# Entry of the down-projection: the order of VectorE's work on low parts of weights, a recombination, a product of convolutions and operands

## The chip, the cores and the metric

The kernel runs on one core of one Trainium2 chip. The metric is the device time of one execution in microseconds (us). Every engine of the core takes its instructions in the order in which the program was laid out for it: TensorE (PE; PEld is its weight load) multiplies matrices, VectorE (DVE) and ScalarE (ACT) work elementwise, GpSimd (POOL) too, and SyncE (SP) issues most transfers. An instruction that must wait for another engine holds up all that stands behind it on its own engine.

## The reference, cut to what matters

One layer of a decoder on 1024 tokens of width 1024. After the attention part, with `x` the residual stream:

```
xn = rmsnorm(x, norm_ffn_w)
u  = xn @ w_up                       # 1024 x 5632
c  = conv_b + sum_j upad[:, j:j+S] * conv_w[j]     # causal, width 3, per channel
gate, val = split(c, 2)
x  = x + (silu(gate) * val) @ w_down # 2816 -> 1024
return rmsnorm(x, norm_final_w)
```

All data are float32. The change touches the seam between `u`, `c` and the product with `w_down`.

## The kernel before, in words

The kernel holds everything transposed: channels on the 128 partitions, tokens along the free axis. A float32 product is made from three matmuls: each operand is split into a high part (a cast by ScalarE, `wh` for weights at line 139, `h` for activations at line 820) and a low part (the rest, by VectorE, `wl` at line 141 and `h` at line 821), and TensorE adds high x high, high x low and low x high.

**The up-projection** (`hidden`) goes over 22 pairs of output blocks j = 0 to 21; NF is 22. Each pair is made by seven products P1 to P7 of half the size, put together by VectorE in `recombine` (lines 460 to 467): `us` of the gate block and `us` of the value block come out of it. GpSimd multiplies `us` by the row scale of the norm (`scaled`, L1051), ScalarE and VectorE do the convolution (`conv`: L1065, L1067, L1068), ScalarE the silu (L1043), VectorE the product of gate and value (`glu`, L1044), and SyncE stores it in DRAM (`hd`, L1045). The work of the value block of the pair before the last, and of both blocks of the last pair, is kept in a list (`self.defer`) and done later, during the down-projection's first chains.

**The down-projection** (`down`) is again made of seven half-size products, the stages P1, P2, P5, P6, P3, P7 and P4. In every stage the 11 blocks k of the inner dimension are cut into six and five; for each cut there are four weights, one for each block of 128 output channels. So i counts 56 weights, and i = 0 to 3 are weights 1 to 4 of stage P1 with six k, i = 4 to 7 weights 5 to 8 with five k. For every weight there is one chain of matmuls (L1121): high x high, high x low, low x high for each k. The activations of P1's first six k are split ahead of it; those of the other five k and of all later stages are the "operands": they are read back from `hd` by `fetch_h` (L1003), combined and split into parts by `operand` while the chains run, two or so at a time. The list `preps` names them in order, and the table `count` says how many follow each weight.

Weights have three buffers as they come from DRAM (`raw`), and two each for the high and the low parts: the cast of weight n + 2 waits until chain n is done, and the load of weight n + 3 until the low part of weight n has been made. SyncE's queue carries, in one order, these loads (L129), the reads of `hd` (L1003), the stores into `hd` (L1045) and the loads of the residual (L1158), which VectorE adds to the chains' results (L1127).

What sets the order on an engine: a planner goes through the program and always issues, on each engine, the ready instruction of the highest priority by its own estimate of times; earlier in the text is higher, and `tc.high_priority(n)` lifts a block. `tc.issue_after(ins)` puts all that a block issues on the engine of `ins` behind `ins`. In this place:

```
with tc.high_priority(100):          # last pair, before its recombine: weights 1 and 2
    for k in range(6, HK):
        self.fetch_h("B11", k)
    self.ahead(2)
self.front = self.hi.ins, self.lo.ins
self.defer.pop(0)(lo)
```

`self.hi` and `self.lo` are the cast and the low part issued last, here those of weight 2; `front` puts the next convolution behind them. In `down`, `next_w` at weight i = 1 prepares weight 3, at i = 2 weight 4, and so on; the operands that follow it stand behind that weight's cast and low part. `DEFER = (2, 4)` and `STORE = (1, 6)` name the i at which the last pair's convolutions and the two late stores are done.

Of the kernel before, what the change touches and what calls it, by code (L numbers as in the profile page):

```python
# [13 lines left out]
ALU = mybir.AluOpType  # L14
# [10 lines left out]
NF = DFF // P  # L25
# [19 lines left out]
class Trunk:  # L45
# [405 lines left out]
                        self.keep(m, u, (tp, "hi"))  # L451
        self.uw = None

    def recombine(self, ps, us, tp, o):

        nc = self.nc
        c11, c12, c21, c22 = (us[w][:, o + hf * H2:o + (hf + 1) * H2] for w in range(2) for hf in range(2))
        s1, u2, u3, u4 = (self.tl(tp, [P, H2], n, bufs=1) for n in ("s1", "u2", "u3", "u4"))
        tt = nc.vector.tensor_tensor
        nc.scalar.copy(s1, ps["P1"])  # L460
        tt(c11, ps["P2"], s1, ALU.add)
        tt(u2, ps["P6"], s1, ALU.add)
        tt(u3, ps["P7"], u2, ALU.add)
        tt(c22, ps["P5"], u3, ALU.add)
        tt(u4, ps["P5"], u2, ALU.add)
        tt(c12, ps["P3"], u4, ALU.add)  # L466
        tt(c21, u3, ps["P4"], ALU.subtract)

    def keep(self, m, u, to):

# [77 lines left out]
    def store(self, dst, src):  # L548

        self.stores.append((dst, src))  # L550
# [353 lines left out]
    def hidden(self, pair):  # L904
        nc, tc = self.nc, self.tc
        with ExitStack() as ctx:
# [11 lines left out]
            for j in range(NF):  # L918
                w, ps = ready.pop(j) if j else (w0, {})
                if j == 0:  # L920
# [4 lines left out]
                    for k in range(4):  # L925
                        hi, lo = self.split(*(xc2.tile([P, T], F32R, name=f"T42_{k}{p}") for p in "hl"), self.t42[k])
                        self.B["T4", k], self.B["T2", k] = ((hi[:, c], lo[:, c]) for c in (slice(0, H2), slice(H2, T)))
                    self.tctx.close()
                    tp = e(tc.tile_pool(name="tp", bufs=2, side="right", reuse_waits="tile"))
# [7 lines left out]
                if j == NF - 1:  # L937
# [3 lines left out]
                    with tc.high_priority(50):  # L941
# [3 lines left out]
                        lo = self.lo  # L945
# [4 lines left out]
                us = [self.tl(tp, [P, T + 2], "us", bufs=3) for _ in range(2)]  # L950
                if j == NF - 1:
# [7 lines left out]
                        self.ahead(2)  # L959
                    self.front = self.hi.ins, self.lo.ins  # L960
                    self.defer.pop(0)(lo)
                self.recombine(ps, us, tp, 2)
                if j < NF - 1:

                    with nullcontext() if j else tc.issue_after(self.pow.ins):

                        w, ps = ready[j + 1] = self.next_w(), {}
# [68 lines left out]
    def glu(self, j, w, us, tp, after):  # L1036

        nc = self.nc
        c = self.conv(j + w * NF, us, tp, after)
        if w == 0:  # L1040
            self.c0 = c
            return
        nc.scalar.activation(self.c0, self.c0, AF.Silu)  # L1043
        nc.vector.tensor_tensor(self.c0, self.c0, c, ALU.mult)  # L1044
        store = lambda c0=self.c0: nc.sync.dma_start(self.hd[j], c0)  # L1045
        self.late.append(store) if after is not None else store()

    def scaled(self, m, us, after=None):
# [22 lines left out]
    def down(self):  # L1071

        nc, tc = self.nc, self.tc
        with ExitStack() as ctx:
# [5 lines left out]
            tt = nc.vector.tensor_tensor  # L1080
# [7 lines left out]
            def fetch(name, *ks):  # L1088
                for k in ks:
                    self.fetch_h(name, k)  # L1090

            def prep(c):
                for _ in range(c):
                    if preps and preps[0] not in (("P4", k) for k, _ in again):
                        stage, k = preps.pop(0)
                        self.operand(stage, k)
                        if stage == "P7":
                            again.append((k, None))
# [16 lines left out]
            def product(ps, w, stage, c, start, a=0, b=H2, each=None):  # L1115

                k0, k1 = CUTS[c]
                for k in range(k0, k1):
                    h, l = (t[:, a:b] for t in self.B[stage, k])
                    for i, (v, x) in enumerate(((w[0], h), (w[0], l), (w[1], h))):  # L1120
                        nc.tensor.matmul(ps, v[:, k - k0, :], x, start=start and k == i == 0, stop=k == HK - 1 and i == 2, skip_group_check=True)  # L1121
                    if each:
                        each(k)

            def evict(ps, m, hf, done):
                x = col(m, hf)
                tt(x, x, ps, ALU.subtract if m > 3 else ALU.add)  # L1127
                if done:
                    norm(m, hf)
# [7 lines left out]
                loads.setdefault(14 + k // 2, []).append(("B22", k))  # L1137
            for k in range(1, 6):
                loads[7 + k].insert(0, ("B11", k))
            count = {0: 3, 1: 2, 3: 1, 4: 1, 6: 2, 7: 2}  # L1140
            chains, owed, tail, i = [{}, {}], [], [], 0
            for stage in STAGES:
                which, start, o, hf, done = plan[stage]
                for c in range(2):
                    for m in range(4):
                        if stage == "P4" and c == 1 and m > 1:
                            break
                        with tc.high_priority(150 if i < 4 else 0), tc.issue_after(self.load.ins) if i == 1 else nullcontext():
                            w = self.next_w()
                        lo = self.lo  # L1150
                        if start and c == 0:
                            chains[which][m] = bank(which)
                        ps = chains[which][m]
                        product(ps, w, stage, c, start)
                        if i % 8 == 2 and i < 32:
                            r, h = ((0, 0), (4, 1), (0, 1), (4, 0))[i // 8]
                            with tc.issue_after(self.load.ins):
                                nc.sync.dma_start(x3[:, r:r + 4, h * H2:(h + 1) * H2], self.x2d[r:r + 4, :, h * H2:(h + 1) * H2].rearrange("m p t -> p m t"))  # L1158
                        for l in loads.get(i, ()):
                            fetch(*l)  # L1160
                        for k, _ in again:
                            fetch("B21", k)
                        again.clear()
                        with tc.issue_after(self.hi.ins), tc.issue_after(lo.ins):
                            prep(count.get(i, 0) if i < 8 else 2 if i % 4 < 2 or i < 16 else 1)
                        if i in DEFER:
                            self.scaled(NF - 1, self.us[len(self.defer) % 2], lo)
                        if i - 1 in DEFER:
                            self.front = self.hi.ins, lo.ins
                            self.defer.pop(0)(lo)  # L1170
                        if i in STORE:

                            with tc.issue_after(self.load.ins):
                                self.late.pop(0)()
                        for f in owed:
                            f()
                        owed = []
                        if c:
                            owed = [lambda ps=ps, m=m + o, hf=hf, done=done: evict(ps, m, hf, done)]
                        if stage == "P4":  # L1180
                            if c == m == 0:
                                tail = self.last_norm(psD, [acc[0][:, 1]], x3, H2, 0, H2, ((0, 2, nc.vector), (6, 8, nc.gpsimd), (2, 4, nc.vector), (4, 6, nc.vector)))
                            elif tail:
                                tail.pop(0)()
                        i += 1
            assert not preps and not again
            ws = [self.next_w() for _ in range(2)]
            for a, b in ((0, q), (q, H2)):
                for m, w in zip((2, 3), ws):
                    ps = chains[1][m][:, a:b]  # L1190
# [117 lines left out]
```

## Time and profile before

| | us |
|---|---|
| median of 3 runs | 1328.85 |
| lowest and highest | 1328.23, 1329.53 |
| the profiled execution, its own time | 1328.35 |
| span of its profile | 1326.6 |
| TensorE busy | 1309.5 |
| VectorE busy | 1057.2 |
| ScalarE busy | 621.1 |
| GpSimd busy | 480.4 |

In the rows of a timeline the first number is the start in us from the start of the span, the second the duration; then come the engine, the line of the kernel, the operation, what it writes and reads, and how many instructions were merged into the row. Square brackets hold the engine's idle time ahead of the row and what ended it. In a row of waits stand the engine and line that waited, what it waited for, and the total, the number and the longest of these waits. The last pair's matmuls end at 1099.8 us of the span, where the down-projection's begin; its own end is the end of the span, 227 us later.

### The profile page before, as it was taken

The numbers are of one execution on the slowest core, as the hardware profiler recorded it, in microseconds if no ns is written. First come the engines' busy times: TensorE is split into PE (matmuls) and PEld (weight loads), VectorE is DVE, ScalarE is ACT, GpSimd is POOL, SyncE is SP. The second block draws the span as 40 slices with busy tenths as digits, with TensorE's granted clock in tenths as the row PEclk, the third lists the DMA queues.
The fourth block names the chain that finished last, engine by engine and source line by source line (L and its number), as shares of the span: only waits on it lengthen the run. The fifth ranks groups of instructions, "written<-read, shape, count | busy, mean of one in ns | idle before, by whom it ended". The sixth has DMA issues, their size and how long they took to land. (4 is left out here: it accounts for less than half of the span.)

```text
span 1326.6 us, 17120 instructions
## 1 busy us (share of the span) xinstructions
PE 1309.5 (99%) x6210; PEld 1088.9 (82%) x6210; DVE 1057.2 (80%) x1456; ACT 621.1 (47%) x967; POOL 480.4 (36%) x364
## 2 busy tenths in 40 slices
PE   9999999999999999999999999999999999999997
PEld 7888888888888878888888888888888787888886
DVE  8846775289888976445669999999999998896865
ACT  8532232276667764333444433343343435554543
POOL 0446652000111015651435657766767641000002
PEclk9999999999999999999999999999999999999999
DMA  7334443976554235334423435564536226963534
GB/s 261 120 143 158 145 148 127 265 183 184 150 129 136 85 132 211 136 111 159 133 105 132 174 123 149 141 210 135 157 138 167 77 86 234 339 198 117 166 98 147
DMA packets 71588, 205.96 MB, mean 155 GB/s; under 512 B 8016, under 2 KB 15824, under 8 KB 71376
## 3 DMA queue, kind: packets, MB, share of 16 engines
q1 hardware_dynamic: 57472, 176.03, 39.6%
q0 software_dynamic: 2304, 11.54, 4.6%
q10 hardware_dynamic: 11728, 17.31, 3.6%
q8 instruction: 49, 0.80, 0.3%
q14 instruction: 35, 0.29, 0.1%
HBM read 156.08 MB, written 71.83 MB: 172 GB/s over the span
## 5 line engine op out<-in xcount | busy, mean ns | idle before, releaser
L141 DVE TENSOR_TENSOR wl<-raw,wh 128x1024 fp32r<-128x1024 f32 (+2 forms) x85 | 97.3, 1146 | 56.4 <-ACT wh L139 46.8
L139 ACT CAST wh<-raw 128x1024 fp32r<-128x1024 f32 (+2 forms) x85 | 74.2, 874 | 113.3 <-PE y L1121 49.4
L1051 POOL TENSOR_TENSOR us<-us,rstd 128x1024 f32<-128x1024 f32 x42 | 93.1, 2277 | 51.8 <-DVE us L466 32.7
L1065 ACT ACTIVATE c<-us,vecs 128x1024 f32<-128x1024 f32 x44 | 54.8, 1247 | 115.5 <-POOL us L1051 109.9
L120 DVE TENSOR_TENSOR sl<-sf,sh 128x1024 fp32r<-128x1024 f32 x62 | 92.7, 1496 | 15.6 <-ACT sh L118 15.6
L118 ACT CAST sh<-sf 128x1024 fp32r<-128x1024 f32 x62 | 64.7, 1045 | 83.8 <-PE t L901 44.0
L104 POOL TENSOR_TENSOR sf<-rv 128x512 f32<-128x512 f32 x30 | 58.0, 1935 | 116.6 <-DVE sl L120 51.1
L177 POOL TENSOR_TENSOR rs<-ms,mhalf 128x8 f32<-128x8 f32 (+2 forms) x9 | 13.3, 1474 | 234.4 <-DVE ms L175 228.3
L1121 PE MATMUL y<-h,wh 128*128 128x512 f32 (+1 forms) x324 | 95.1, 377 | 0.0
L1121 PE MATMUL d<-h,wh 128*128 128x512 f32 x264 | 81.3, 389 | 0.0
L1068 DVE SCALAR_TENSOR_TENSOR c<-us,vecs,c 128x1024 f32<-128x1024 f32 x44 | 75.4, 1746 | 0.1
L160 PE MATMUL g<-xh,wh 128*128 128x512 f32 x176 | 70.9, 403 | 1.5 <-ACT g L562 1.5
L161 PE MATMUL g<-xl,wh 128*128 128x512 f32 x176 | 70.3, 400 | 0.0
L162 PE MATMUL g<-xh,wl 128*128 128x512 f32 x176 | 70.3, 399 | 0.0
L120 DVE TENSOR_TENSOR wl<-raw,wh 128x1024 fp32r<-128x1024 f32 (+1 forms) x32 | 69.1, 2159 | 0.1
L1121 PEld LDWEIGHTS y<-h,wh 128*128 128x128 f32 x324 | 59.4, 188 | 11.0
L106 POOL TENSOR_TENSOR sf<-raw,rv 128x512 f32<-128x512 f32 x30 | 54.0, 1798 | 36.8 <-DVE sl L120 36.8
L1067 DVE SCALAR_TENSOR_TENSOR c<-us,vecs,c 128x1024 f32<-128x1024 f32 x44 | 63.0, 1464 | 1.6 <-ACT c L1065 1.5
L637 DVE CUSTOM_DVE_ANT_0 L<-sc,bias 128x128 f32<-128x128 f32 (+7 forms) x64 | 47.7, 751 | 17.0 <-PE sc L633 13.7
L616 POOL MEMSET aT<- 128x128 f32 x32 | 6.2, 206 | 151.7 <-PE t L662 98.0
L1121 PE MATMUL y<-h,wl 128*128 128x512 f32 (+1 forms) x162 | 60.9, 376 | 0.0
L638 ACT ACTIVATE L<-L,sm 128x128 f32<-128x128 f32 (+7 forms) x64 | 49.6, 778 | 20.0 <-DVE sm L637 17.3
(394 smaller groups left out, 4156.1 us busy)
## 6 DMA issues: line engine op xcount, KB each, us to landing
u<-qd SPq DMA_DIRECT2D x72, 256.0 KB, 6.3
raw<-in_w_up SPq DMA_DIRECT2D x23, 512.0 KB, 5.0
raw<-in_w_in SPq DMA_DIRECT2D x22, 512.0 KB, 3.8
hd<-c SPq DMA_DIRECT2D x22, 512.0 KB, 2.6
sdP<-in_w_down POOLq DMA_DIRECT2D x16, 704.0 KB, 9.0
rv<-in_w_up SPq DMA_DIRECT2D x21, 512.0 KB, 4.6
hc<-hd SPq DMA_DIRECT2D x33, 256.0 KB, 5.0
gr<-gd SPq DMA_DIRECT2D x16, 512.0 KB, 3.5
```

The lines of the kernel that those rows point to most:

```text
L104: tt(sa[:, 0], v[:, 0], v[:, 1], ALU.add)
L118: cast = nc.scalar.copy(hi, src)
L120: low = nc.vector.tensor_tensor(lo, src, hi.bitcast(F32), ALU.subtract)
L139: self.hi = nc.scalar.copy(wh, raw)
L141: self.lo = (eng or nc.vector).tensor_tensor(wl, raw, wh.bitcast(F32), ALU.subtract)
L160: nc.tensor.matmul(ps, wh[:, kc + o, :], ah, start=first and n == 0, stop=False)
L161: nc.tensor.matmul(ps, wh[:, kc + o, :], al, start=False, stop=False)
L162: nc.tensor.matmul(ps, wl[:, kc + o, :], ah, start=False, stop=last and n == len(kcs) - 1)
L1051: i = (nc.vector if m % NF == 0 else nc.gpsimd).tensor_tensor(us[:, 2:], us[:, 2:], self.rstd, ALU.mult)
L1067: nc.vector.scalar_tensor_tensor(c, us[:, 1:T + 1], cw[1], c, ALU.mult, ALU.add)
L1068: nc.vector.scalar_tensor_tensor(c, us[:, 0:T], cw[0], c, ALU.mult, ALU.add)
L1121: nc.tensor.matmul(ps, v[:, k - k0, :], x, start=start and k == i == 0, stop=k == HK - 1 and i == 2, skip_group_check=True)
```

## The change

Three edits, all in the order of work around the start of the down-projection. No operation is added or taken away.

1. `recombine` takes an instruction `after`, and for the last pair its last two sums, c12 and c21 (L466 and L467), are queued behind the low part issued last, that of weight 2.
2. The product of gate and value (L1044) of the two late stores is no longer made in `glu`; it is made together with the store, at i = 1 for the pair before the last and at i = 6 for the last pair, and queued behind the low part of the weight prepared there (weight 3 and weight 8). The transfer stays behind the loads issued before it, as it was.
3. `count` changes: after weight i = 0, 1, 2, 3, 4, 6, 7 came 3, 2, 0, 1, 1, 2, 2 operands; now 0, 2, 2, 1, 2, 2, 2. The sum is 11 in both.

```
-    def recombine(self, ps, us, tp, o):
+    def recombine(self, ps, us, tp, o, after=None):
...
-        tt(c12, ps["P3"], u4, ALU.add)
-        tt(c21, u3, ps["P4"], ALU.subtract)
+        with self.tc.issue_after(after) if after is not None else nullcontext():
+            tt(c12, ps["P3"], u4, ALU.add)
+            tt(c21, u3, ps["P4"], ALU.subtract)
...
-                self.recombine(ps, us, tp, 2)
+                self.recombine(ps, us, tp, 2, self.lo.ins if j == NF - 1 else None)
...
         nc.scalar.activation(self.c0, self.c0, AF.Silu)
-        nc.vector.tensor_tensor(self.c0, self.c0, c, ALU.mult)
-        store = lambda c0=self.c0: nc.sync.dma_start(self.hd[j], c0)
+
+        def store(c0=self.c0):
+            nc.vector.tensor_tensor(c0, c0, c, ALU.mult)
+            nc.sync.dma_start(self.hd[j], c0)
+
         self.late.append(store) if after is not None else store()
...
-            count = {0: 3, 1: 2, 3: 1, 4: 1, 6: 2, 7: 2}
+            count = {1: 2, 2: 2, 3: 1, 4: 2, 6: 2, 7: 2}
...
-                            with tc.issue_after(self.load.ins):
+                            with tc.issue_after(self.load.ins), tc.issue_after(lo.ins):
                                 self.late.pop(0)()
```

## The prediction

> **What bounds the kernel now.** I read the page first, then the chain of work that ended last, then what TensorE waited for, and last the engines' timelines around the place where the second and the third meet.
>
> ```profile
> PE 1309.5 (99%) x6210; PEld 1088.9 (82%) x6210; DVE 1057.2 (80%) x1456; ACT 621.1 (47%) x967; POOL 480.4 (36%) x364
> ```
>
> ```profile
> 1111.18 0.88 DVE wl L141
> ...
> 1112.10 21.62 PE y L1121 x94
> ...
> 1317.09 0.02 issue
> ```
>
> ```profile
> PE y L1121 <- DVE wl L141: 3.2, 2, 2.6
> ```
>
> The first line is the page's: TensorE is busy in 99% of the 1326.6 us. The next rows are the chain, followed back from the end: from 1112.10 us to 1317.09 us it holds TensorE's work alone, and what released that run is VectorE's low part of a weight (`wl`, line 141). So whatever brings the matmul at 1112.10 us forward brings the end forward by as much, if no new gap opens behind it. The last row is from the list of TensorE's waits: the down-projection's matmuls (L1121) waited twice for that low part, 3.2 us in all, 2.6 the longer; it is TensorE's largest entry.
>
> TensorE's timeline shows both gaps. A weight serves one chain of matmuls, three for each k; I number the weights of the first stage 1 to 8. Weights 1 to 4 have six k (18 matmuls), weights 5 to 8 five k (15). Chains 2 to 5 begin at the rows with two matmuls:
>
> ```profile
> 1103.89 0.63 PE L1121 MATMUL y<-sh,wh 128*128 128x512 f32 x2
> 1105.07 0.50 PE L1121 MATMUL y<-sh,wl 128*128 128x512 f32 x1 [0.55 <-DVE wl L141]
> ...
> 1108.85 0.61 PE L1121 MATMUL y<-sh,wh 128*128 128x512 f32 x2
> 1112.10 0.50 PE L1121 MATMUL y<-sh,wl 128*128 128x512 f32 x1 [2.64 <-DVE wl L141]
> ...
> 1115.88 0.62 PE L1121 MATMUL y<-sh,wh 128*128 128x512 f32 x2
> 1116.33 0.39 PE L1121 MATMUL y<-sh,wl 128*128 128x512 f32 x1
> ...
> 1119.96 0.62 PE L1121 MATMUL y<-h,wh 128*128 128x512 f32 x2
> ```
>
> The undisturbed fourth chain lasts 1119.96 - 1115.88 = 4.08 us. The second lasts 1108.85 - 1103.89 = 4.96 and the third 1115.88 - 1108.85 = 7.03: 0.88 and 2.95 too long, 3.83 us together. This is more than the 3.2 of the waits, since the idle time is counted only from the modelled end of the matmul before. In a chain that does not wait, the first matmul with `wl` starts 0.45 us behind the chain's start (1116.33 - 1115.88); there it is 1.18 and 3.25.
>
> Why `wl` comes late is in VectorE's timeline, with the casts of ScalarE that it needs:
>
> ```profile
> 1102.88 0.68 DVE L465 TENSOR_TENSOR u<-t,u 128x512 f32<-128x512 f32 x1
> 1103.48 0.68 DVE L467 TENSOR_TENSOR us<-u,t 128x512 f32<-128x512 f32 x1
> 1104.07 0.95 DVE L141 TENSOR_TENSOR wl<-raw,wh 128x768 fp32r<-128x768 f32 x1
> 1105.03 1.29 DVE L1067 SCALAR_TENSOR_TENSOR c<-us,vecs,c 128x1024 f32<-128x1024 f32 x1
> 1106.23 0.69 DVE L466 TENSOR_TENSOR us<-t,u 128x512 f32<-128x512 f32 x1
> 1106.83 1.28 DVE L1068 SCALAR_TENSOR_TENSOR c<-us,vecs,c 128x1024 f32<-128x1024 f32 x1
> 1108.15 1.23 DVE L1044 TENSOR_TENSOR c<-c,c 128x1024 f32<-128x1024 f32 x1
> 1109.29 1.89 DVE L821 TENSOR_TENSOR h<-ha,h 128x512 fp32r<-128x512 f32 x3
> 1111.10 0.95 DVE L141 TENSOR_TENSOR wl<-raw,wh 128x768 fp32r<-128x768 f32 x1
> 1111.96 1.28 DVE L821 TENSOR_TENSOR h<-ha,h 128x512 fp32r<-128x512 f32 x2
> ...
> 1116.62 0.82 DVE L141 TENSOR_TENSOR wl<-raw,wh 128x640 fp32r<-128x640 f32 x1 [2.50 <-ACT wh L139]
> ...
> 1126.96 1.28 DVE L1068 SCALAR_TENSOR_TENSOR c<-us,vecs,c 128x1024 f32<-128x1024 f32 x1
> 1128.17 0.82 DVE L141 TENSOR_TENSOR wl<-raw,wh 128x640 fp32r<-128x640 f32 x1
> ```
>
> ```profile
> 1100.40 0.83 ACT L139 CAST wh<-raw 128x768 fp32r<-128x768 f32 x1
> 1103.75 1.25 ACT L1065 ACTIVATE c<-us,vecs 128x1024 f32<-128x1024 f32 x1 [2.52 <-POOL us L1051]
> 1104.90 1.65 ACT L820 CAST h<-ha 128x512 fp32r<-128x512 f32 x3
> 1106.46 0.83 ACT L139 CAST wh<-raw 128x768 fp32r<-128x768 f32 x1
> ```
>
> The casts of weights 2 and 3 end at 1101.23 and 1107.29; their low parts start at 1104.07 and 1111.10. Neither waits for data: VectorE works without a break from one to the other, on things that TensorE does not need yet.
>
> **The change, part by part.** *The last two sums of the recombination* (L466, L467) go behind weight 2's low part. L465 is followed at 1103.48; the low part takes that start, ends at 1103.48 + 0.95 = 1104.43, and TensorE goes on 0.05 later (it ended at 1105.02 and TensorE resumed at 1105.07), at 1104.48, against 1103.89 + 0.45 = 1104.34 without any wait. Of the first gap some 0.14 us and the restart stay. L467 then has 1104.34 to 1105.02 (a start follows 0.86 behind this low part's, as 1111.96 - 1111.10), just the time in which VectorE would wait for L1065 (1103.75 + 1.25 = 1105.00). So L1067 stays at 1105.03, L466 at 1106.23, L1068 at 1106.83: this swap costs nothing, because the wait for ScalarE covers it. What reads these sums is GpSimd's multiply of the last pair, which waits for weight 4's low part anyway (row below).
>
> *The product* L1044 of the pair before the last becomes part of the store and goes behind weight 3's low part, as do *the operands*: no pair of parts after weight 1, two each after the low parts of weights 3 and 4, one after 5, two after 6, instead of three ahead of weight 3. What stood between L1068 and weight 3's low part was 1.23 and 1.89 busy us: with both gone the low part can start one step behind L1068, 1.21 us (the distance from L1068 to L141 in the rows 1126.96 and 1128.17), thus at 1106.83 + 1.21 = 1108.04. Its cast is no later than before (1107.29), and ScalarE has three casts (1.65 us) fewer ahead of it. It ends at 1108.99, and TensorE resumes at 1109.04 instead of 1112.10: **3.06 us earlier**. A wait of about 0.4 us remains, as this chain would want it at about 1104.48 + 4.08 = 1108.56.
>
> *Upper bound.* If the order puts weight 3's low part ahead of L1068, it ends by 1107.8 and no wait is left: the gain is all of 3.83 us. I take 3.06: ahead of this low part the order of before takes all that is ready (seven instructions stand between the two low parts), which tells that the order's own estimate has this cast late, and L1068 is neither moved nor held by the change.
>
> *What is late next.* All of this is relative to TensorE, 3.06 earlier. Weight 4's low part needs weight 2's chain done; behind weight 3's come two operands (1.28) and the product (1.23), so it runs from 1108.04 + 0.86 + 1.21 + 1.2 = 1111.3 to 1112.3, and it is wanted at 1116.33 - 3.06 = 1113.27: 1.0 us spare. The cover for the moved work is thus VectorE's idle 2.50 us ahead of 1116.62, where it waits for a cast that waits for TensorE. The two operands that come after weight 4 fit there, and they are wanted a whole chain later, from 1119.96 - 3.06 on.
>
> *Queues.* SyncE loads raw weights in the order of the low parts, and operands and stores stand behind them:
>
> ```profile
> 1105.05 7.36 SPq L129 DMA_DIRECT2D raw<-in_w_down  x2
> 1112.46 2.71 SPq L1003 DMA_DIRECT2D hc<-hd  x3
> 1115.22 0.43 SPq L1045 DMA_DIRECT2D hd<-c  x1
> ...
> 1116.22 0.97 SPq L1158 DMA_DIRECT2D x<-x2d  x1
> ```
>
> ```profile
> 1114.20 2.00 POOL L1051 TENSOR_TENSOR us<-us,rstd 128x1024 f32<-128x1024 f32 x1 [10.48 <-DVE wl L141]
> ```
>
> ```profile
> 1124.31 0.69 DVE L1127 TENSOR_TENSOR x<-x,y 128x512 f32<-128x512 f32 x1 [2.08 <-DMA x<-x2d]
> 1124.91 0.82 DVE L141 TENSOR_TENSOR wl<-raw,wh 128x640 fp32r<-128x640 f32 x1
> ```
>
> The second load of the first row waits until 1112.05, when weight 3's low part has read its buffer. It goes with that low part, 3.06 earlier, and three operand loads behind it. The store now waits for the product: done by about 1111.3, against its turn at 1115.22 - 3.06 = 1112.16, so it holds nothing up. The residual's load (L1158) comes at about 1113.2, and the eviction that waits for it, with weight 7's low part behind it (1124.91), keeps its distance to TensorE. No transfer is added. The product of the last pair, behind weight 8's low part now, stood behind it already: zero.
>
> **The sum**: 3.06 us off the profiled execution's 1328.35 (span 1326.6), that is 1325.29; the median of the runs shown is 0.50 above this execution, so 1328.85 - 3.06 = **1325.8**, 0.23% less. 0.2%, or 2.66 us, is about what a measurement of this kernel can tell from no change.
>
> **Rivals.** *All of it*: weight 3's low part is put ahead of L1068: 1328.85 - 3.83 = 1325.0. For it speaks that its cast would be done by 1106; against it, the order of before. 0.14.
>
> *Part given back to a shared port.* GpSimd's last-pair multiply ran while VectorE stood idle (1114.20 to 1116.20). Now it starts behind weight 4's low part at 1112.3, beside two operands.
>
> ```profile
> 1073.63 4.41 POOL L1051 TENSOR_TENSOR us<-us,rstd 128x1024 f32<-128x1024 f32 x2 [2.08 <-DVE us L466]
> 1076.87 1.73 DVE L821 TENSOR_TENSOR rv<-sf,rv 128x512 fp32r<-128x512 f32 x1 [0.69 <-ACT rv L820]
> ```
>
> Beside such a multiply the same operation took 1.73 us, against 1.89 / 3 = 0.63 a piece in the row of three. Two operands so slowed last 3.4 us, from 1112.2 to 1115.6; weight 5's low part (0.82) then ends at 1116.4, wanted at 1119.96 - 3.06 + 0.45 = 1117.35; one operand, L1067 and L1068 (0.6 + 1.2 + 1.2) and weight 6's low part bring VectorE to 1120.3, wanted at 1117.35 + 3.40 = 1120.75 (a chain of 15 matmuls takes 15/18 of 4.08). It decides from 0.4 us more, as when L1067 is slowed too (another 1.1 to 1.4): up to 1 us comes back, 1326.8. 0.10. [...]
>
> *The store blocks SyncE* (slower). The product now decides when SyncE passes the store, and the loads of weight 7 and the residual stand behind it. If the order puts the product behind weight 6's low part (about 1118.5), it ends at 1119.7, the residual's load goes at 1120.8, lands 8.1 later (1116.22 to 1124.31) at 1128.9, and the eviction and weight 7's low part end 0.6 + 0.8 later, at 1130.4. TensorE in the profile of before wants it in chain 7, at 1119.96 + 2 x 3.40 + 0.45 = 1127.21: 3.2 late, 1332.0. It decides once the residual's load goes later than 1116.22 + 1.48 (the spare of that low part then, 1127.21 - 1125.73), that is with a product that ends later than 1116.6. Against it: the product's inputs are ready before 1108.2. 0.09.
>
> *The change does nothing*: weight 3's low part is still placed last, as its cast waits for the first chain's buffer: 1328.85. Against it: the operands may not pass it now. 0.09.
>
> **How the numbers follow.** The forecast has 0.58. Its gain lies only 0.4 us over the bound, about what medians of few runs move (1328.23 to 1329.53 here), so it gives 0.46 faster and 0.12 the same; all of it 0.14 faster; the port 0.02 and 0.08; nothing, 0.08 the same and 0.01 slower; the store 0.09 slower. That is 0.62, 0.28, 0.10. The likeliest alone has 1325.1 to 1326.6. The range takes in the full gain with 0.5 for the runs, 1324.5, and the port's case and beyond, up to 1328.4.
>
> **What would show it.** Right: the wait of L1121 for `wl` falls from 3.2 us to about 0.5; chain two takes about 4.2 us, chain three about 4.5; L1044 stands behind the third `wl` and ahead of the fourth; the residual's load goes at about 1113. Wrong: a new wait of L1121 for a `wl` behind weight 3, operands over 1.5 us beside L1051, or a store that starts after 1113.

## The result, and the profile after

The changed kernel takes 1324.63 us in the median of six runs (1323.31 to 1325.13), the kernel before 1328.9; the ratio is 0.9964, with a 95% interval of 0.9951 to 0.9977. A second comparison gave 1326.74 against 1329.65, ratio 0.9975 (0.9965 to 0.9985). So it is faster, by 3.3 us (2.0 to 4.7) by the second ratio and 4.8 us (3.1 to 6.5) by the first, where 3.06 was forecast. The first ratio, taken on the 1328.85 us of the kernel before, gives 1324.1 us: 1.7 us under the forecast of 1325.8, and under the range's low end of 1324.5. It says more than the 3.83 us that the prediction held for the most, though its interval reaches down to 3.1.

In the changed kernel the lines have moved: the matmuls are L1125 (L1121 before), the operands' low parts L822 (L821), the convolution L1071 and L1072 (L1067, L1068), the product L1047 (L1044), the last sums L467 and L468 (L466, L467), GpSimd's multiply L1055 (L1051), the eviction L1131 (L1127). VectorE's timeline at the seam, in the first profile of the changed kernel:

```profile
1100.33 0.68 DVE L465 TENSOR_TENSOR u<-t,u 128x512 f32<-128x512 f32 x1
1100.93 1.05 DVE L141 TENSOR_TENSOR wl<-raw,wh 128x768 fp32r<-128x768 f32 x1
1101.90 0.67 DVE L468 TENSOR_TENSOR us<-u,t 128x512 f32<-128x512 f32 x1
1102.50 1.27 DVE L1071 SCALAR_TENSOR_TENSOR c<-us,vecs,c 128x1024 f32<-128x1024 f32 x1
1103.70 0.68 DVE L467 TENSOR_TENSOR us<-t,u 128x512 f32<-128x512 f32 x1
1104.30 1.27 DVE L1072 SCALAR_TENSOR_TENSOR c<-us,vecs,c 128x1024 f32<-128x1024 f32 x1
1105.49 0.94 DVE L141 TENSOR_TENSOR wl<-raw,wh 128x768 fp32r<-128x768 f32 x1
1106.36 1.28 DVE L822 TENSOR_TENSOR h<-ha,h 128x512 fp32r<-128x512 f32 x2
1107.56 1.22 DVE L1047 TENSOR_TENSOR c<-c,c 128x1024 f32<-128x1024 f32 x1
1108.70 0.95 DVE L141 TENSOR_TENSOR wl<-raw,wh 128x768 fp32r<-128x768 f32 x1
```

The order is the one forecast, instruction by instruction: low part 2 behind L465, low part 3 one step (1.19 us) behind the second pass of the convolution, then two operands, the product, low part 4. TensorE's timeline of the same execution:

```profile
1097.61 0.62 PE L1125 MATMUL y<-sh,wh 128*128 128x512 f32 x2
...
1101.69 0.62 PE L1125 MATMUL y<-sh,wh 128*128 128x512 f32 x2
...
1105.81 0.61 PE L1125 MATMUL y<-sh,wh 128*128 128x512 f32 x2
1106.49 0.50 PE L1125 MATMUL y<-sh,wl 128*128 128x512 f32 x1
...
1110.25 0.62 PE L1125 MATMUL y<-sh,wh 128*128 128x512 f32 x2
...
1114.33 0.62 PE L1125 MATMUL y<-h,wh 128*128 128x512 f32 x2
```

Chain 2 lasts 4.12 us (4.96 before), chain 3 4.44 (7.03). The two waits for `wl` have left the list of TensorE's waits; one of 0.6 us has come, in the stage P5, with a wait of ScalarE for a raw weight that leads to it (VectorE is idle for 2.65 us behind ScalarE, and then works without a break up to that low part):

```profile
PE d L1125 <- DVE wl L141: 0.6, 1, 0.6
ACT wh L139 <- DMA raw<-in_w_down: 2.6, 1, 2.6
```

But this pair of profiles does not add up by itself. The down-projection starts at 1097.61 here and at 1099.81 in the profile of before, so 2.20 of the 3.2 us between the spans lie ahead of every edited instruction; chains 1 to 4 are 3.43 shorter (16.72 instead of 20.15); and what follows is 2.4 longer (209.0 instead of 206.6). Three questions: is the earlier start the change's? What gives gain back later? And why do the times say more than the seam can give?

### The profile page after: what moved, and what is told of

It is laid out like the page before. It is cut to its first block, busy times and chain, and to the rows that moved or that the text cites. A ratio compares the mean times of both kernels' runs of the same rounds, so it can differ in the third digit from the quotient of the medians.

```text
span 1323.3 us, 17121 instructions
## 1 busy us (share of the span) xinstructions
PE 1310.0 (99%) x6210; PEld 1089.0 (82%) x6210; DVE 1059.7 (80%) x1456; ACT 621.7 (47%) x967; POOL 480.4 (36%) x364
## 4 chain that ended last, share of the span: by engine, by line
PE 76%; DVE 11%; issue 5%; DMA 4%; POOL 2%; ACT 1%; SPq 0%; POOLq 0%; DVEq 0%; ACTq 0%
PE t L902 27%; PE y L1125 8%; PE d L1125 4%; PE g L160 4%; PE g L161 4%; PE g L162 4%; PE sc L161 3%; PE sc L160 3%; PE sc L162 3%; PE sc L634 3%; DVE c L1071 2%; DVE wl L120 2%; DVE c L1072 2%; PE t L650 1%; DMA rv<-in_w_up 1%
## 5 line engine op out<-in xcount | busy, mean ns | idle before, releaser
L1055 POOL TENSOR_TENSOR us<-us,rstd 128x1024 f32<-128x1024 f32 x42 | 94.8, 2290 | 48.0 <-DVE us L467 31.5
L104 POOL TENSOR_TENSOR sf<-rv 128x512 f32<-128x512 f32 x30 | 54.6, 1819 | 116.6 <-DMA rv<-in_w_up 56.4
L1125 PE MATMUL y<-h,wh 128*128 128x512 f32 (+1 forms) x324 | 95.1, 377 | 0.0
L1125 PE MATMUL d<-h,wh 128*128 128x512 f32 x264 | 81.2, 389 | 0.0
L1072 DVE SCALAR_TENSOR_TENSOR c<-us,vecs,c 128x1024 f32<-128x1024 f32 x44 | 75.4, 1746 | 0.1
L1125 PEld LDWEIGHTS y<-h,wh 128*128 128x128 f32 x324 | 59.4, 188 | 11.0
L1071 DVE SCALAR_TENSOR_TENSOR c<-us,vecs,c 128x1024 f32<-128x1024 f32 x44 | 64.3, 1490 | 1.8 <-ACT c L1069 1.7
L120 DVE TENSOR_TENSOR wl<-raw,wh 128x1024 fp32r<-128x1024 f32 (+1 forms) x32 | 62.8, 1963 | 0.1
L1125 PE MATMUL y<-h,wl 128*128 128x512 f32 (+1 forms) x162 | 61.1, 377 | 0.0
```

The source lines that it names most:

```text
L120: low = nc.vector.tensor_tensor(lo, src, hi.bitcast(F32), ALU.subtract)
L1055: i = (nc.vector if m % NF == 0 else nc.gpsimd).tensor_tensor(us[:, 2:], us[:, 2:], self.rstd, ALU.mult)
L1071: nc.vector.scalar_tensor_tensor(c, us[:, 1:T + 1], cw[1], c, ALU.mult, ALU.add)
L1072: nc.vector.scalar_tensor_tensor(c, us[:, 0:T], cw[0], c, ALU.mult, ALU.add)
```

## The experiments

Each profile is read by three lengths: the start of the down-projection (its first matmul), chains 1 to 4 from there, and the rest up to the end of the span. In the tables below all are differences of TensorE's rows, as above; "behind P5" is what lies from the first matmul of the stage P6 to the end of the span.

### The two kernels again

No edit.

> The kernel before, once more, to tell what an execution varies by in the part that no edit touches. If the 2.2 us by which the changed kernel reached the down-projection earlier (first matmul of L1121 at 1097.61 instead of 1099.81) is a matter of the execution, this run's first matmul comes anywhere from 1097 to 1101 and the two waits of TensorE for L462 (1.3 us in all before) come and go. If it belongs to the program, it comes at 1099.8 within 0.3, with both waits. From the first matmul to the end: 226.8 us within 0.4 either way. Ratio 1.000.

> The changed kernel once more. From the first matmul of the down-projection to the end 225.7 us within 0.4 (226.8 before), whatever the start. If the earlier start is a matter of the execution, the first matmul comes anywhere from 1097 to 1101 and the ratio is nearer to 0.998 than to 0.996; if it belongs to the program, it comes at 1097.6 within 0.3 and the ratio stays at 0.996 to 0.997.

| kernel | start | chains 1 to 4 | chains 5 to 8 | stages P2 and P5 | behind P5 | from the start to the end |
|---|---|---|---|---|---|---|
| before, first profile | 1099.81 | 20.15 | 13.60 | 60.09 | 132.9 | 226.8 |
| before, again | 1101.13 | 21.79 | 13.60 | 60.09 | 133.3 | 228.8 |
| changed, first profile | 1097.61 | 16.72 | 13.96 | 61.75 | 133.3 | 225.7 |
| changed, again | 1101.05 | 17.13 | 13.87 | 60.40 | 132.9 | 224.3 |

The kernel before came to 1330.06 us, ratio 1.0004 (0.9995 to 1.0013); the changed one has the second comparison above. The start is a matter of the execution: the same changed program reached the down-projection at 1097.61 and at 1101.05. In all 14 profiles of this case, none of which has an edit ahead of the last pair, it comes between 1097.6 and 1101.1. So an execution can differ by the 2.20 us without any change. The late raw load of the first profile did not come back either: here TensorE has no wait for it, and from the start to the end it takes 224.3 us, 2.4 less than the first profile of before (the run was expected at 225.7, as in the first profile of the changed kernel): 3.02 gained in chains 1 to 4 (3.06 forecast) and 0.58 given back in chains 5 to 8 and the stages P2 and P5. Chains 2 to 5 begin here at

```profile
1105.13 0.62 PE L1125 MATMUL y<-sh,wh 128*128 128x512 f32 x2
...
1109.60 0.61 PE L1125 MATMUL y<-sh,wh 128*128 128x512 f32 x2
...
1114.10 0.62 PE L1125 MATMUL y<-sh,wh 128*128 128x512 f32 x2
...
1118.18 0.62 PE L1125 MATMUL y<-h,wh 128*128 128x512 f32 x2
```

Chain 2 takes 4.47 us and chain 3 4.50, and in the four later kernels with all of the change they take 4.45 to 4.49. The 4.12 of chain 2 in the first profile, near the 4.2 of the forecast, did not come again. Low part 2 takes 1.05 us in all six (0.95 before), beside a multiply of GpSimd that is still running (in the first profile to 1101.17); low part 3 starts 8.22 to 8.25 us behind the first matmul in five of them, where 1108.04 - 1099.81 = 8.23 was forecast (7.88 in the first profile).

The surprise is the kernel before: 2.0 us more than in its first profile, 1.64 of it in chains 1 to 4 (the other 0.4 behind P5, where both kernels have it in one of their profiles). Its timeline behind the long wait, and the view by windows (busy time of the engines, then the granted clock of TensorE, the DMA's share and its GB/s):

```profile
1113.44 0.50 PE L1121 MATMUL y<-sh,wl 128*128 128x512 f32 x1 [2.65 <-DVE wl L141]
1113.78 0.63 PE L1121 MATMUL y<-sl,wh 128*128 128x512 f32 x2
1114.25 0.54 PE L1121 MATMUL y<-sl,wl 128*128 128x512 f32 x1
1114.58 1.06 PE L1121 MATMUL y<-rv,wh 128*128 128x512 f32 x2
1115.44 0.63 PE L1121 MATMUL y<-rv,wl 128*128 128x512 f32 x1
1115.86 1.06 PE L1121 MATMUL y<-rv,wh 128*128 128x512 f32 x2
...
1117.89 0.39 PE L1121 MATMUL y<-sh,wl 128*128 128x512 f32 x1
```

```profile
1112.00:1114.00 2.00, 0.56 (x2) 0.48 (x3) 2.00 (x4) 0.00 (x0) 0.00 (x0) 1.00 0.00 0
1114.00:1116.00 2.00, 2.00 (x7) 1.56 (x6) 1.46 (x2) 0.00 (x0) 0.46 (x1) 0.58 0.75 215
1116.00:1118.00 2.00, 2.00 (x7) 1.59 (x6) 0.00 (x0) 0.00 (x0) 1.54 (x1) 0.56 1.02 312
1118.00:1120.00 2.00, 2.00 (x11) 1.60 (x10) 0.45 (x1) 1.21 (x3) 0.00 (x0) 1.00 1.10 393
```

The wait is the same 2.65 us, but about 1 us behind it the clock falls to 0.58 and 0.56, seven matmuls take the 2 us in which eleven fit, and at 1118 it is back. In the first profile of before the clock stayed at 1.00 there. So in this execution the same wait cost 1.64 us more than in the other. The two kernels with a longer wait below have such a fall once each in their profiles. Worked out from the windows of 2 us, the clock is at 0.50 for about 3.4 us in all three; the fall begins 0.9 and 1.3 us behind the end of the wait in two of them and 0.5 us ahead of it in the third. What decides whether an execution has the fall, and where it begins, is not shown.

The mean clock that each run lists tells how often it was low: of 85 runs of the kernel before in these comparisons, 32 have 0.996 or less, and these take 1331.1 us in the mean against 1329.3 for the other 53. Of the 60 runs of kernels whose longest wait here is 1.4 us or less (all below but the three with long waits) none has. The mean is a coarse measure: 4 us at 0.55 take only 0.0014 from it, and the profile of the kernel with the longer wait below has such a fall at a mean of 0.997, so the 32 need not be all.

### Is it the idle time that lets the clock fall?

Three kernels made from the kernel before. Two lengthen the wait; the first makes three low parts twice, the second five times (`range(4)`):

```
         self.B[stage, k] = self.parts_h(a)
+        if stage == "P1" and k < 9:
+            h, l = self.B[stage, k]
+            tt(l, a, h.bitcast(F32), ALU.subtract)
```

> The kernel before with TensorE's second wait made longer: VectorE makes the low parts of the three operands ahead of weight 3 twice (the same values again), three instructions of 0.6 us, so that the wait of 2.65 us becomes about 4.4. If a wait of this kind costs only its own length, chain 3 takes 7.03 + 1.8 = 8.8 us, the matmuls behind it run at the full clock, and the median lies 1.8 us above the kernel before. If TensorE's granted clock falls behind a long wait, as in the profile of the second run of the kernel before (0.58 and 0.56 from 1114 to 1118 us, 2.0 us lost), the clock falls here in nearly every execution: matmuls at twice their spacing behind the wait, mean clocks of 0.996 and less in most runs, and a median 3 to 4.5 us above the kernel before.

> The kernel before with VectorE making the low parts of three operands five times (the same values again), so that TensorE's wait ahead of weight 3's low part becomes 7 to 10 us. If the granted clock falls when TensorE has been idle for some microseconds at an unlucky moment, this wait is long enough to contain that moment always: the clock is about 0.5 behind the wait in the profile, the mean clock is under 0.997 in every one of the runs, and the time is above the kernel before by the longer wait and 1.5 to 2 us more. If the low clock in some runs of the kernel before has nothing to do with the wait, the clocks are mixed as there (about a third at 0.996 and less).

The third fills it:

```
                     for i, (v, x) in enumerate(((w[0], h), (w[0], l), (w[1], h))):
+                        if idle and k == 0 and i == 2:
+                            for n in range(11):
+                                nc.tensor.matmul(idle[0], w[0][:, 0, :], h, start=n == 0, stop=n == 10)
...
-                        product(ps, w, stage, c, start)
+                        product(ps, w, stage, c, start, idle=[bank(0)] if i == 2 else None)
```

> The kernel before with eleven matmuls more (11 x 0.23 = 2.5 us), on data that is there, whose result nothing reads, put between the second and the third matmul of chain 3, where TensorE otherwise waits 2.65 us for weight 3's low part. They fit into the wait, so chain 3 keeps its 7.0 us. If it is the idleness of this wait that lets the granted clock fall, the clock stays at 1.0 behind it, no run has a mean clock of 0.996 or less (25 of 70 runs of the kernel before have), and the median lies 0.5 to 1 us under the kernel before. If the clock falls for another reason, about a third of the runs still show 0.996 or less and the median is the same or, with the added matmuls, above.

| kernel | TensorE's long wait | runs with a mean clock of 0.996 or less | median, before beside it | ratio |
|---|---|---|---|---|
| longer wait | 3.85 us | 4 of 11 | 1331.62, 1329.84 | 1.0012 (1.0003 to 1.0021) |
| longest wait | 3.84 us, and 2.03 later | 5 of 5 | 1335.41, 1330.24 | 1.0041 (1.0026 to 1.0055) |
| filled wait | none | 0 of 11 (7 of 15 before) | 1328.85, 1330.35 | 0.9991 (0.9982 to 1.0000) |

Both lengthened kernels missed their sizes: the order put weight 3's low part ahead of one of the three repeated ones in the first and of nine of the twelve in the second, so the wait grew by 1.2 us only, and the second got another wait of 2.03 us in chain 6 (5.85 us instead of 3.40; three matmuls take 0.68 us behind it, as ahead of it). The first is inconclusive by its runs (4 of 11, where "most" was expected), though its profile, at a mean clock of 0.997, has the fall:

```profile
1112.00:1114.00 2.00, 0.00 (x0) 0.00 (x0) 2.00 (x4) 0.00 (x0) 0.00 (x0) 0.97 0.00 0
1114.00:1116.00 2.00, 1.62 (x4) 1.33 (x5) 2.00 (x4) 0.00 (x0) 0.00 (x0) 0.50 0.29 44
1116.00:1118.00 2.00, 2.00 (x8) 1.58 (x7) 1.00 (x2) 0.00 (x0) 0.92 (x1) 0.67 0.95 362
```

The filled wait decides. In its trace TensorE multiplies through the wait, and nothing else about the wait has changed: low part 3 comes as late as before, chain 3 starts at 1108.04 and the chain's third matmul 3.25 us later.

```profile
1108.04 0.62 PE L1124 MATMUL y<-sh,wh 128*128 128x512 f32 x2
1108.49 2.65 PE L1123 MATMUL d<-sh,wh 128*128 128x512 f32 x11
1111.29 0.50 PE L1124 MATMUL y<-sh,wl 128*128 128x512 f32 x1
```

The low mean clocks are gone (0 of 11 runs, 7 of 15 of the kernel before beside them), and the kernel is no slower with eleven useless matmuls: the ratio has it faster by 0.0009 (0 to 0.0018), about 1.2 us. So in this kernel it is the idleness of that wait. The price of the long wait is its length and, on the average of the executions, an estimated 0.7 us (32 of 85 times 1.8) to 1.2 us; the interval of the filled kernel allows 0 to 2.4.

### The three parts of the change

Each part of the diff alone, on the kernel before, and the last two without the first:

```
# only operands
-            count = {0: 3, 1: 2, 3: 1, 4: 1, 6: 2, 7: 2}
+            count = {1: 2, 2: 2, 3: 1, 4: 2, 6: 2, 7: 2}
# only product
+        def store(c0=self.c0):
+            nc.vector.tensor_tensor(c0, c0, c, ALU.mult)
+            nc.sync.dma_start(self.hd[j], c0)
...
+                            with tc.issue_after(self.load.ins), tc.issue_after(lo.ins):
# product and operands: both of these
```

> Of the change only the operands' new places; the product stays ahead of weight 3's low part, the recombination as before. By the prediction's steps weight 3's low part starts the three operands (1.81 us) earlier: chain 3 takes 7.03 - 1.8 = 5.2 us, chain 2 still 4.96. From the first matmul to the end 1.8 us less the 0.5 that later stages give back: about 225.5. If the clock falls only behind long waits, this wait of about 0.9 us leaves it whole, every run has a mean clock of 0.997 or more, and the median is 2 to 2.5 us under the kernel before; if not, 1.3.

> Of the change only the product's new place; three operands stay ahead of weight 3's low part. That low part starts one product (1.14 us) earlier: chain 3 takes about 5.9 us, TensorE's wait is 1.5 us instead of 2.65, chain 2 still 4.96. From the first matmul to the end about 225.9. With a clock that falls only behind long waits the mean clock stays at 0.997 or more in all runs, and the median lies 1.3 to 2 us under the kernel before; with a clock that falls behind shorter waits too, some runs show 0.996 and less.

> The change without its first part: the last two sums of the recombination stay ahead of weight 2's low part. By the prediction's steps this part is worth nothing in the end: chain 2 stays at 4.96 us instead of 4.12, chain 3 takes some 0.8 less than the 4.44 of the changed kernel, and weight 3's low part starts as long behind the first matmul (7.9 us) as in the changed kernel. A rival, that the shorter chain 2 is a gain of its own: 0.5 to 0.8 us longer from the first matmul to the end.

| kernel | chain 2 | chain 3 | chains 1 to 4 | chains 5 to 8, P2, P5 | ratio |
|---|---|---|---|---|---|
| only operands | 4.96 | 5.2 | 18.34 | 73.74 | 0.9975 (0.9960 to 0.9989) |
| only product | 4.96 | 5.8 | 18.89 | 73.84 | 0.9980 (0.9970 to 0.9990) |
| product and operands | 4.97 | 4.1 | 17.21 | 74.13 | 0.9975 (0.9965 to 0.9986) |
| whole change, again | 4.47 | 4.50 | 17.13 | 74.27 | 0.9975 (0.9965 to 0.9985) |

Against chains 1 to 4 of the kernel before (20.15), the operands bring 1.81 (1.81 expected), the product 1.26 (1.14), both 2.94. The first part adds 0.08: without it the wait stays in chain 2 and goes from chain 3, because low part 3 stands at the same place behind L1068. That it is worth nothing held. The ratios can't tell these kernels apart. By their middle values the parts that shorten chain 3 by 1.3 and 1.8 us win 2.7 us (1.3 to 4.0) and 3.3 us (1.5 to 5.3), more than the lengths of one profile; the intervals still hold 1.3 and 1.8. None of their 17 runs has a clock of 0.996 or less, so with the wait cut to 1.4 us (operands left ahead) or 0.8 us no fall shows in the mean clocks any more.

### What gives 0.58 us back?

In the first profile of the changed kernel SyncE issued the second residual load ahead of weight 13's raw load, behind it before. One edit puts it back, and moves no other engine's instruction:

```
-                            with tc.issue_after(self.load.ins):
+                            with tc.issue_after((self.raws[-2] if i == 10 else self.load).ins):
                                 nc.sync.dma_start(x3[:, r:r + 4, ...], self.x2d[...])
```

> The changed kernel with one transfer in another place: SyncE issues the second load of the residual behind weight 13's raw load, as before the change, and not ahead of it; nothing else moves on any engine. If this megabyte ahead of the raw load is what gives back part of the gain, ScalarE's wait of 2.6 us for that load goes, VectorE's idle 2.65 us behind it too, TensorE's lost time in the stages P2 and P5 falls from about 1.8 to under 0.6 us, and from the first matmul to the end it takes about 224.3 us. If VectorE is simply full there, the waits stay at 1.5 us or more and the end at 225.7.

1327.18 us, ratio 0.9979 (0.9970 to 0.9988); chains 5 to 8 13.87, P2 and P5 60.39, from the start to the end 224.3, just as expected. But this is what the changed kernel without this edit had in its second profile, with the same two waits of TensorE of some 0.24 us, at the low parts of weights 7 and 9. So the explanation falls though its number came: the order of these two loads does nothing by itself, and the late landing was that execution's.

The second try was the number of operands ahead of weight 7:

```
-            count = {1: 2, 2: 2, 3: 1, 4: 2, 6: 2, 7: 2}
+            count = {1: 2, 2: 2, 3: 2, 4: 1, 6: 2, 7: 2}
```

> The changed kernel with two operands behind weight 5 and one behind weight 6, instead of one and two. In the changed kernel the two behind weight 6 run beside GpSimd's multiply (3.09 us instead of 1.28) ahead of the eviction and of weight 7's low part, and TensorE waits 0.2 to 0.3 us in chain 7. If that is the cause, the wait goes and chains 5 to 8 take 13.65 us instead of 13.9; if weight 7's low part is late for the residual's load, it stays. In the median 0.25 us less than the changed kernel, too little to be told apart by times.

1326.29 us, ratio 0.9976 (0.9965 to 0.9987). The wait at weight 7 goes, that at weight 9 grows to 0.39: chains 5 to 8 take 13.75 (13.65 expected), P2 and P5 60.56, to the end 224.3. It only moves the shortage. What is short is VectorE's time, and the changed kernel's second profile shows where it goes:

```profile
1114.84 2.36 DVE L141 TENSOR_TENSOR wl<-raw,wh 128x640 fp32r<-128x640 f32 x1 [0.18 <-ACT wh L139]
...
1121.09 3.10 DVE L822 TENSOR_TENSOR h<-hc,h 128x512 fp32r<-128x512 f32 x2
1124.10 0.68 DVE L1131 TENSOR_TENSOR x<-x,y 128x512 f32<-128x512 f32 x1
1124.70 0.81 DVE L141 TENSOR_TENSOR wl<-raw,wh 128x640 fp32r<-128x640 f32 x1
```

```profile
1113.53 2.98 POOL L1055 TENSOR_TENSOR us<-us,rstd 128x1024 f32<-128x1024 f32 x1 [8.56 <-DVE wl L141]
1121.25 2.39 POOL L1055 TENSOR_TENSOR us<-us,rstd 128x1024 f32<-128x1024 f32 x1 [4.74 <-DVE wl L141]
```

Weight 5's low part takes 2.36 us (0.82 before), two operands 3.10 (1.28). GpSimd's multiply of the last pair runs beside both. What counts is where it ends: the low part ends at 1117.20, 0.69 us behind the first multiply's end (1116.51), the second operand at 1124.19, 0.55 us behind the second one's (1123.64), so each ended behind GpSimd by 0.13 us less than it takes undisturbed (0.82 and 0.68 us). What holds them up beside GpSimd is not shown. One kernel leaves this multiply out, so its last pair is unscaled; the other does it on VectorE:

```
# no multiply
+        if m % NF == NF - 1:
+            return
# on VectorE
-        i = (nc.vector if m % NF == 0 else nc.gpsimd).tensor_tensor(us[:, 2:], us[:, 2:], self.rstd, ALU.mult)
+        i = (nc.vector if m % NF in (0, NF - 1) and after is not None or m % NF == 0 else nc.gpsimd).tensor_tensor(...)
```

> The changed kernel without GpSimd's multiply of the last pair by the row scale (L1055, two instructions): this leaves that multiply out, so the last pair's hidden channels are unscaled. In the changed kernel the low part of weight 5 beside the first of them takes 2.41 us (0.82 else) and two operands beside the second 3.09 (1.28 else): 3.4 us of VectorE. If that is what makes the low parts of weights 7 and 9 late, they take 0.82 and 1.28 here, TensorE's two waits of 0.24 us each go, chains 5 to 8 take 13.6 and the stages P2 and P5 together 60.1 (13.87 and 60.40 in the changed kernel), and from the first matmul to the end it takes 223.8 us. If VectorE is late there for its own work alone, the waits stay at 0.2 us each.

> The changed kernel with the same two multiplies on VectorE instead of GpSimd, at the same places. VectorE gets two instructions of about 1.2 us more, and loses nothing to GpSimd: 2.4 us against 3.4, so if the two engines stand in each other's way, VectorE is 1.0 us ahead of the changed kernel behind weight 6, the waits at weights 7 and 9 shrink to 0.2 us together, and from the first matmul to the end it takes 224.1 us. If they do not, VectorE is 2.4 us later and the waits at weights 7 and 9 grow to 1 us or more: 225.5 us or more.

| kernel | chains 1 to 4 | chains 5 to 8 | P2 and P5 | behind P5 | start to end | ratio |
|---|---|---|---|---|---|---|
| no multiply | 17.07 | 13.60 | 60.09 | 133.3 | 224.1 | 0.9963 (0.9950 to 0.9976) |
| multiply on VectorE | 17.06 | 13.60 | 60.11 | 133.3 | 224.1 | 0.9965 (0.9953 to 0.9978) |

VectorE's rows with the multiply in its own queue:

```profile
1112.96 1.22 DVE L1055 TENSOR_TENSOR us<-us,rstd 128x1024 f32<-128x1024 f32 x1
1114.09 0.81 DVE L141 TENSOR_TENSOR wl<-raw,wh 128x640 fp32r<-128x640 f32 x1
...
1118.75 1.29 DVE L822 TENSOR_TENSOR h<-hc,h 128x512 fp32r<-128x512 f32 x2
1119.95 1.22 DVE L1055 TENSOR_TENSOR us<-us,rstd 128x1024 f32<-128x1024 f32 x1
1121.09 0.68 DVE L1131 TENSOR_TENSOR x<-x,y 128x512 f32<-128x512 f32 x1
1121.68 0.82 DVE L141 TENSOR_TENSOR wl<-raw,wh 128x640 fp32r<-128x640 f32 x1
```

Both waits are gone, in both kernels: chains 5 to 8 and the two stages are back at the lengths of the kernel before. VectorE does 2.44 us more and is still earlier, because 2.36 + 3.10 us shrink to 0.81 + 1.29. So the 0.58 us is GpSimd's multiply beside VectorE, as in the prediction's rival of the port, only at weights 7 and 9, not 5 and 6. The kernel with the multiply on VectorE has the shortest way from the start to the end of all complete ones here, 224.1 against 224.3, though the profiles of both kernels here have the longer 133.3 us behind P5 (the changed kernel's second has 132.9): TensorE's last four matmuls (L183) take 1.11 us in both and 0.65 in the changed kernel's second profile. In the first profiles the same four take 1.11 us where the window of 2 us has a granted clock of 0.50 (changed kernel, 1316 to 1318 us), and 0.65 where it has 1.00 (before, 1320 to 1322). By times the gain is less than can be told (0.9965 and 0.9975 come from different chips, and their intervals overlap).

## Why the prediction was right or wrong

- *The bound, the two gaps, their cause*: right. VectorE's order was the cause, and the low parts went where the prediction put them.
- *The last two sums, worth nothing*: right (0.08 us). Low part 2 took 0.10 us longer beside GpSimd's multiply (1.05 instead of 0.95), which the sum does not hold, but this took nothing off the gain: low part 3 started where it was forecast.
- *The product and the operands, 3.06 us at weight 3*: right. Chains 1 to 4 are 3.02 shorter in the profile without a disturbance, and each part alone brings its own share.
- *"Upper bound ... the gain is all of 3.83 us"*: wrong, and this is the step that failed. It priced the long wait at its own length, from one profile in which the clock stayed at 1.00 behind it. In the second profile of before it fell to 0.58 and 0.56; 32 of 85 runs of that kernel have a mean clock of 0.996 or less, and these took 1.8 us longer. With the wait cut to 1.4 us or less none of 60 runs has such a mean clock: an estimated 0.7 to 1.2 us in the mean, a term that the sum put at nothing. The range's low end, 1324.5, is that bound with 0.5 us for the runs, and the first ratio goes 0.4 us beyond it.
- *"with 0.5 for the runs"*: too little for what lies ahead of the edited instructions. The start of the down-projection moved by 3.4 us from one execution of the changed kernel to another, and in the first pair of profiles 2.20 us of the difference lie there.
- *"keeps its distance to TensorE"*: wrong by 0.58 us. The spare of weights 7 and 9 was used up by GpSimd's multiply, which before ran while VectorE was idle. The rival of the port had this slowing, two weights too early. No run shows a port; they show low parts of 2.36 us (0.82 undisturbed) and 3.10 for two (1.28) beside that multiply. It was told as a rival, and it came along with the forecast instead of in its place. Two of the three signs that were to show the prediction wrong did appear: small waits for low parts behind weight 3, and operands of 3.10 us for two beside the multiply.
- *SyncE, the store, the raw loads*: right that they hold nothing up. The late raw load of one profile was not the change's.
- *The sum*: 3.06 forecast; 3.0 - 0.6 + 0.7 to 1.2 by the runs gives 3.1 to 3.6, against 3.3 us (2.0 to 4.7) and 4.8 (3.1 to 6.5) by the two ratios. That the second lies so near the forecast is luck in part: what was given back and the price of the clock, both missing from the sum, nearly cancel. The 1.2 to 1.7 us by which the first exceeds 3.1 to 3.6 have no cause shown. The earlier start of the down-projection in that comparison's profile of the changed kernel would cover them, but why it was earlier there stays open.

## What to carry to other kernels

Price a wait of TensorE by its length, and look besides at the granted clock in short windows behind each wait of some microseconds, in more than one execution: here a wait of 2.65 us cost 1.64 us more in the one whose clock fell to 0.58 and 0.56. Before moving work into an engine's idle time, look at what ran beside that idle time: here it was GpSimd's multiply, beside which VectorE's low part of a weight took 2.36 us instead of 0.82. And compare two profiles from the first edited instruction on, not by their spans: here the start of the down-projection moved by 3.4 us from one execution of the same kernel to another.

## What the runs showed of the hardware

Behind a wait of TensorE of 2.65 us the granted clock fell to 0.58 and 0.56 in two windows of 2 us in one profile of the kernel before, from about 0.9 us behind the wait's end (about 3.4 us at 0.50, an estimate from these windows); in the other, with 2.64 us, it stayed at 1.00. Of 11 runs with that wait filled by matmuls none had a mean clock of 0.996 or less, of 15 of the kernel before beside them 7; with waits of 0.8 and 1.4 us none of 17. Beside a GpSimd multiply a low part of a weight (128x640) took VectorE 2.36 us instead of 0.82, and two of operands (128x512) took 3.10 instead of 1.28; they ended 0.69 and 0.55 us behind the multiply's end. The same multiply on VectorE took 1.22 us, less than the 1.54 and 1.82 that VectorE lost beside it on GpSimd.
